# Layer 0's conditioning sums, all eight groups, split between TensorE's column quarters and VectorE

## Chip, cores and metric

The kernel runs on one NeuronCore of a Trainium2 chip. The metric is the device time of one execution in microseconds (us). Engines are named as in the profile: PE is TensorE's matmul, PEld its weight load, DVE is VectorE, ACT is ScalarE, POOL is GpSimd, SP is SyncE, which here only issues transfers.

## What is computed

A trunk of two layers over 256 tokens of width 2048. Each layer normalises its input twice, and each norm is scaled and shifted by vectors that come from a conditioning vector `c`:

```
cond = jax.nn.silu(c)
for l in range(DEPTH):
    mod = cond @ w_ada[l] + b_ada[l]
    shift1, scale1, gate1, shift2, scale2, gate2 = [m[:, None, :] for m in jnp.split(mod, 6, axis=-1)]
    h = rms_norm(x, norm1_w[l]) * (1.0 + scale1) + shift1
    mixed = mixer_groups(h, positions, w_in[l], ...)
    x = x + gate1 * (mixed @ w_out[l])
    h = rms_norm(x, norm2_w[l]) * (1.0 + scale2) + shift2
    gate_up = h @ w_ffn_in[l]
    ...
    x = x + gate2 * ((jax.nn.silu(g_ff) * u_ff) @ w_ffn_down[l])
return rms_norm(x, final_norm_w)
```

`cond @ w_ada[l]` is a vector of 2048 times a matrix of 2048 x 12288 in float32, 100 MB a layer. All sums are in float32.

## The kernel before

**The large products.** Every product with a large weight is made from two rounded parts of each operand, three matmuls in place of one. A piece of weights (256 rows, up to 512 columns) is loaded into `raw`, one of a ring of nine buffers, by SP; ACT rounds it to `whi` (L268), DVE takes the rest as `wlo` (L269), and PE runs it against `hTh` and `hTl`, the parts of the activations (L380, and L415 with the operands swapped). `fill` keeps LA = 3 pieces prepared ahead of PE; `hlp` has four buffers of each.

**The conditioning sums.** Before, they are no matmuls. For one group of a norm, `ada_pair` covers 512 of the 2048 columns, of the shift and of the scale together, so 1024 sums over 2048 rows. It takes 16 units, one for each 128 rows: unit `k` loads `raw` (128 x 2 x 512, 512 KB), and DVE adds `raw` times `cond[:, k]` to an accumulator `acc` (L443 for the first, L445 for the others). Then the 128 partitions must still be summed: `turn` transposes `acc` in eight blocks on PE (L472), `total_of` reduces on DVE (L478) and adds bias and norm weight (L479, L481). Four groups of a norm, two norms and two layers make 16 such groups. The gates (`ada_gate`, L441) go the same way and are not touched.

**The order.** All is written out in program order; an engine runs its own instructions in that order. Units wait in the queue `bg` and are popped between blocks (`pump`), at a rate set by when their group is due. The first norm of layer 0 has nothing to hide behind: its group 0 is run at once, all 16 units, with the start-up work between them (`setup`). Its groups 1 to 3 run beside the body of the group before: `first_groups` takes group g of the activations through eight column blocks of `w_in` (FIRST), and ahead of body g it calls `require`, which runs `at_once` of that group: the transposes, a `fill`, the reductions. Then `norm_steps` makes `hTh` and `hTl` on ACT (L606, L607) and DVE (L608), and the body starts with L415. The second norm's groups are deferred: their last steps are put between blocks some steps later (`later`).

**Start-up.** `c` is loaded as rows (`rowc`) and turned into columns by a transpose against the 128 x 128 identity `identt`; `silu` of it is `cond`. Transfers of SP and of ACT take semaphores from one ring of eight in turn, so a transfer waits until the one eight places before it in the ring has landed. Consts go through ACT's queue ahead of `cond`.

Of the kernel before, what the change touches and what calls it, by code (L numbers as in the profile page):

```python
# [19 lines left out]
P = 128  # L20
# [4 lines left out]
L = 2  # L25
# [9 lines left out]

LA = 3
NRAW = 9
NBIG = 24

CF = {}  # L40
_o = 0
# [39 lines left out]
def decoder(ctx: ExitStack, tc: tile.TileContext, x_d, c_d, pos_d, w_ada, b_ada, n1_d, w_in, w2_d, b2_d,  # L81
# [39 lines left out]
    nc.scalar.dma_start(identt, cf_d[:, CF["ident"][0]:CF["ident"][1]])  # L121
# [7 lines left out]
    load_rows(nc.scalar, lb_d, "lb")  # L129
    load_rows(nc.scalar, n1_d, "n1")  # L130
    brows = T2([P, P], n="brows")
    for l in range(L):
        for wh in range(2):
            o = 32 * (2 * l + wh)
            nc.scalar.dma_start(brows[o:o + 32],
                                b_ada[l, 6144 * wh:6144 * wh + 4096].rearrange("(r p) -> r p", p=P))
# [284 lines left out]

    def ada(l, c0, pair, finish, defer, dl):
        st = {}
        w = 512 if pair else 1024
        np_ = 1024 // w

        def unit(k):
            if k == 0:  # L430
                st["a"] = T4([P, np_, w], n="acc")
                if not pair:
                    G.memset(st["a"], 0.0)
                    nc.gpsimd.dma_start(st["a"][0:1, 0, :], b_ada[l:l + 1, c0:c0 + w])
            raw = rawp.tile([P, np_, w], F32, tag="raw", name=nm("raw"))
            rows_ = w_ada[l, k * P:(k + 1) * P, :]
# [5 lines left out]
            if pair and k == 0:  # L442
                V.tensor_scalar(out=st["a"], in0=raw, scalar1=cond[:, 0:1], scalar2=None, op0=ALU.mult)  # L443
            else:
                V.scalar_tensor_tensor(out=st["a"], in0=raw, scalar=cond[:, k:k + 1], in1=st["a"], op0=ALU.mult,  # L445
                                       op1=ALU.add)
            if k == KT - 1:
                if defer is None:
                    fill()
                    finish(st["a"])  # L450
                elif defer:
                    later.append([defer, None, lambda: finish(st["a"])])
                else:
                    finish(st["a"])

        for k in range(KT):
            bg.append((dl, lambda k=k: unit(k)))

    def ada_pair(l, which, g, dl, defer=6):
        base = 0 if which == 1 else 6144  # L460
# [13 lines left out]
        def total_of(j):  # L474
# [5 lines left out]
            if j:  # L480
                V.tensor_tensor(out=av[:, c], in0=s, in1=cols[:, r + 4 * g:r + 4 * g + 4], op=ALU.mult)  # L481
                done.add(key)

        def at_once(acc):
            turn(0, acc)
            turn(1, acc)
            fill(LA + 1 if g else LA)
            total_of(0)
            total_of(1)

        def fin(acc):
            def second():
                total_of(0)
                turn(1, acc)

            if defer:
# [8 lines left out]
        ada(l, base + 512 * g, True, fin, defer, dl)  # L505

    gates = {}

# [708 lines left out]
    def first_groups(act, nsteps, l, per_group):  # L1217
# [32 lines left out]
        for g in range(4):  # L1250
# [1 line left out]
            per_group(g)  # L1252
            next(nsteps)
            if g == 0:
                for _ in range(2):
# [39 lines left out]
    def at(W, r0, c0):  # L1295
        return where[W.offset, W.shape, r0, c0]

    for g in range(4):
        ada_pair(0, 1, g, at(w_in[0], g * 512, 4368), 0 if g else None)
    for l in range(L):  # L1300
        if l:
            for g in range(4):
# [5 lines left out]
        for h in range(2):  # L1308
            ada_gate(l, 2, h, at(w_fd[l], 0, 0) - 6)
    def setup():  # L1310
        yield from lower_bounds()
        yield
# [6 lines left out]
        yield  # L1319
        yield from trig()  # L1320

    his, los, xs = [], [], []
    prep = setup()
    for k in range(KT):
        bg.popleft()[1]()
        if k == 0:
            load_rows(nc.gpsimd, n2_d, "n2")
            load_rows(nc.gpsimd, b2_d, "b2")
# [4 lines left out]
        if k >= 2:  # L1333
            next(prep, None)
    nsteps = norm_steps(colv[0, "a1"], colv[0, "s1"], his, los, xs, False)

    def last_blocks(bs, adds, key, nsteps, xs):
# [207 lines left out]
```

## Time and profile before

| | |
|---|---|
| median of 3 runs | 2475.21 us (2473.01 to 2477.68) |
| profiled execution | 2479.04 us, its span 2477.2 us |
| busy over the span | PE 96%, DVE 72%, ACT 46%, POOL 4% |
| HBM read | 621.93 MB |
| instructions on PE (matmuls) | 11903 |

The profiled execution is 1.8 us longer than its span, and 3.8 us above the median of the runs. A busy PE in the profile is not PE at its peak, as the ends of pipelined matmuls are modelled; the pace of matmuls is read from the starts of following rows.

### The profile page before, as it was taken

The page shows a single profiled execution, that of the slowest core. Times are in us where ns is not written, and L with a number is a line of the kernel's source. Part 1 is how long each engine was busy: PE and PEld are TensorE (multiplying, and loading weights), DVE is VectorE, ACT ScalarE, POOL GpSimd, SP SyncE. Part 2 cuts the span into 40 slices and gives each one's busy share as a digit, 9 for nine tenths or more (in the row PEclk, how much of TensorE's full clock was granted, in tenths as well). Part 3 has the DMA queues.
Part 4 walks back from the last instruction along what each step waited for, and adds up shares of the span by engine and source line. Part 5 has one row for each costly group of instructions (what it writes and reads, how often), then busy time and mean ns, then how long its engine had stood idle before and what let it go on. Part 6 is the DMA issues. An engine that isn't in the chain of part 4 may idle for free.

```text
span 2477.2 us, 32091 instructions
## 1 busy us (share of the span) xinstructions
PE 2381.7 (96%) x11903; PEld 2007.2 (81%) x11903; DVE 1790.2 (72%) x2020; ACT 1129.3 (46%) x1560; POOL 99.1 (4%) x93
## 2 busy tenths in 40 slices
PE   2998989999999999999999999999999999999998
PEld 2887778878888888888879998888888888888886
DVE  6899899887777776777776787867876555455556
ACT  4434444455443344344455544554644344433444
POOL 0001220000000000000000111000000000000000
PEclk9999999999999999999999999999999999999999
DMA  8998689987888888888767776677787565555653
GB/s 310 362 340 295 184 262 311 313 290 281 299 280 295 285 273 277 281 274 298 270 224 246 245 227 213 226 233 260 257 277 268 203 194 182 186 196 193 194 199 108
DMA packets 314077, 626.16 MB, mean 253 GB/s; under 512 B 20276, under 2 KB 33568, under 8 KB 313664
## 3 DMA queue, kind: packets, MB, share of 16 engines
q1 hardware_dynamic: 312800, 622.68, 74.0%
q8 instruction: 93, 1.52, 0.3%
q10 hardware_dynamic: 720, 1.21, 0.1%
q14 instruction: 64, 0.52, 0.1%
q0 software_dynamic: 400, 0.22, 0.0%
HBM read 621.93 MB, written 2.10 MB: 252 GB/s over the span
## 4 chain that ended last, share of the span: by engine, by line
PE 74%; DVE 1%; ACT 1%; DMA 0%; issue 0%; ACTq 0%; DVEq 0%
PE d L380 66%; PE d L415 3%; PE d L398 1%; PE m L622 1%; PE m L380 1%; PE m L713 0%; PE m L719 0%; DVE wlo L269 0%; PE m L472 0%; ACT whi L268 0%; PE m L1003 0%; PE o L1045 0%; PE m L594 0%; PE m L885 0%; DMA raw<-in_w_in_dram 0%
## 5 line engine op out<-in xcount | busy, mean ns | idle before, releaser
L269 DVE TENSOR_TENSOR wlo<-raw,whi 128x1024 fp32r<-128x1024 f32 (+2 forms) x816 | 969.0, 1196 | 494.0 <-ACT whi L268 477.8
L268 ACT ACTIVATE whi<-raw 128x1024 fp32r<-128x1024 f32 (+2 forms) x816 | 833.9, 1036 | 779.1 <-PE d L380 646.1
L380 PE MATMUL d<-whi,hTh 128*128 128x512 f32 (+2 forms) x1880 | 503.3, 390 | 3.6 <-ACT whi L268 3.5
L380 PE MATMUL d<-whi,hTl 128*128 128x512 f32 (+2 forms) x1880 | 496.6, 384 | 0.0
L380 PE MATMUL d<-wlo,hTh 128*128 128x512 f32 (+2 forms) x1880 | 492.6, 384 | 0.0
L445 DVE SCALAR_TENSOR_TENSOR acc<-raw,cond,acc 128x1024 f32<-128x1024 f32 x368 | 478.7, 1301 | 7.1 <-DMA raw<-in_w_ada_dram 6.1
L380 PEld LDWEIGHTS d<-wlo,hTh 128*128 128x128 f32 x1880 | 348.8, 189 | 70.2
L380 PEld LDWEIGHTS d<-whi,hTl 128*128 128x128 f32 x1880 | 346.7, 189 | 68.8
L380 PEld LDWEIGHTS d<-whi,hTh 128*128 128x128 f32 x1880 | 341.0, 189 | 69.1 <-ACT whi L268 4.6
L380 PE MATMUL d<-whi,ah 128*128 128x512 f32 x672 | 180.9, 391 | 0.0
L380 PE MATMUL d<-whi,al 128*128 128x512 f32 x672 | 179.8, 389 | 0.0
L380 PE MATMUL d<-wlo,ah 128*128 128x512 f32 x672 | 179.7, 389 | 0.0
L380 PEld LDWEIGHTS d<-wlo,ah 128*128 128x128 f32 x672 | 126.2, 188 | 26.4
L380 PEld LDWEIGHTS d<-whi,al 128*128 128x128 f32 x672 | 126.1, 188 | 26.4
L380 PEld LDWEIGHTS d<-whi,ah 128*128 128x128 f32 x672 | 125.2, 188 | 25.3
L254 ACT ACTIVATE ah<-m 128x512 fp32r<-128x512 f32 x44 | 26.3, 598 | 102.7 <-PE m L622 102.7
L1442 ACT ACTIVATE sg<-d 128x512 f32<-128x512 f32 x44 | 23.9, 596 | 101.6 <-PE d L380 101.6
L1078 DVE TENSOR_TENSOR tmp<-d,gate 128x512 f32<-128x512 f32 x64 | 43.9, 686 | 31.8 <-PE d L380 20.5
L415 PE MATMUL d<-hTh,whi 128*128 128x256 f32 x320 | 50.3, 303 | 15.4 <-ACT hTh L606 15.3
L257 DVE TENSOR_TENSOR al<-m,ah 128x512 fp32r<-128x512 f32 x44 | 30.3, 689 | 46.1 <-ACT ah L254 46.1
L380 PE MATMUL d<-whi,mh 128*128 128x512 f32 x224 | 61.4, 395 | 1.7 <-DVE tmp L1078 1.7
L539 ACT ACTIVATE junk<-x 128x512 f32<-128x512 f32 x44 | 27.7, 630 | 75.1 <-DVE x L1079 75.1
(304 smaller groups left out, 2058.6 us busy)
## 6 DMA issues: line engine op xcount, KB each, us to landing
raw<-in_w_ada_dram SPq DMA_DIRECT2D x384, 512.0 KB, 5.4
raw<-in_w_ffn_in_dram SPq DMA_DIRECT2D x352, 512.0 KB, 4.8
raw<-in_w_in_dram SPq DMA_DIRECT2D x176, 512.0 KB, 5.4
raw<-in_w_ffn_down_dram SPq DMA_DIRECT2D x176, 512.0 KB, 4.9
raw<-in_w_out_dram SPq DMA_DIRECT2D x64, 512.0 KB, 5.5
raw<-in_w_in_dram SPq DMA_DIRECT2D x32, 256.0 KB, 3.6
raw<-in_w_in_dram SPq DMA_DIRECT2D x16, 272.0 KB, 4.1
x<-in_x_dram SPq DMA_DIRECT2D x2, 1024.0 KB, 7.3
```

The lines of the kernel that those rows point to most:

```text
L254: A.activation(hi, src, AF.Copy)
L257: V.tensor_tensor(out=lo, in0=src, in1=hi.bitcast(F32), op=ALU.subtract)
L268: A.activation(hi, raw, AF.Copy)
L269: lows.append(lambda: V.tensor_tensor(out=lo, in0=raw, in1=hi.bitcast(F32), op=ALU.subtract))
L380: TE.matmul(ps[t][:, :w], x4[:, k, t * P:(t + 1) * P], wp[:, kk], start=first and k + n == 0, stop=last and k == 3 and n == 2)
L398: TE.matmul(o, x4[:, k, t * P:(t + 1) * P], wp[:, kk], start=first and k + n == 0, stop=last and k == 3 and n == 2)
L415: TE.matmul(ps[f // 2][:, (f % 2) * S:(f % 2 + 1) * S], wp[:, kk, f * P:(f + 1) * P], x4[:, k], start=first and k + n == 0 and f % 2 == 0, ...
L445: V.scalar_tensor_tensor(out=st["a"], in0=raw, scalar=cond[:, k:k + 1], in1=st["a"], op0=ALU.mult, op1=ALU.add)
L539: A.activation(junk, xt[t][:, c * 512:(c + 1) * 512], AF.Square, accum_out=ssq[:, t, c:c + 1])
L622: TE.transpose(ps[:, h], y[:, h * P:(h + 1) * P], ident)
L1078: V.tensor_tensor(out=tmp, in0=ps, in1=gt, op=ALU.mult)
L1442: A.activation(s_, pg[t], AF.Silu)
```

## The change

For the eight groups of layer 0's two norms, part of the 16 units of a group goes to PE. `quarters` is a float32 matmul in four parts: the stationary operand is a column of `cond` widened to 32 columns by zeros (`wide[:, k]`), the moving operand a quarter of `raw` (256 of its 1024 columns), and the output of quarter j lies on PSUM partitions 32j to 32j + 31, so that it uses the array's columns 32j to 32j + 31. One call is one unit, called a set below. Its sum over the 128 rows is done by the matmul itself.

- Group 0 of the first norm (`first_group`): units 1, 3, 5, 7, 9 stay on DVE, the other eleven go to PE and accumulate in one PSUM bank; DVE's accumulator is added there by one more set against a column of ones.
- The other seven groups: units 1, 2, 6, 7, 11, 12 go to PE, in pairs. A pair is two sets that follow each other in a PSUM buffer of their own (a visit, below); DVE copies or adds its 128 x 256 result to `part` (L468, L470 of the changed kernel). Ten units stay on DVE. At the end one set against ones folds `acc` (`folded`), DVE adds `part` (`row_sums`), and `columns` turns the result with two transposes in place of eight and adds bias and weight with three short DVE operations.
- `cond` is made with a 16 x 16 identity loaded by itself, and the other consts are loaded behind it.
- The square sums of x come ahead of `lower_bounds` in `setup`; `setup` starts one unit later.
- Four units in place of two are popped at the start of body 0; one big buffer less (NBIG 23).

```
-NBIG = 24
+NBIG = 23
...
+    ident16 = con.tile([KT, KT], F32, name="ident16")
+    nc.scalar.dma_start(ident16, cf_d[0:KT, CF["ident"][0]:CF["ident"][0] + KT])
...
-    TE.transpose(cond_ps, rowc, ident[:KT, :KT])
+    TE.transpose(cond_ps, rowc, ident16)
     cond = con.tile([P, KT], F32, name="cond")
     A.activation(cond, cond_ps, AF.Silu)
+    wide = con.tile([P, KT + 1, 32], F32, name="wide")
+    parts2 = con.tile([P, 2, 256], F32, name="part")
+    V.memset(wide, 0.0)
+    V.tensor_copy(wide[:, 0:KT, 0], cond)
+    V.tensor_copy(wide[:, KT, 0:1], ones)
+    load_consts()
...
+    def quarters(ps, k, src, first, last):
+        for j in range(4):
+            TE.matmul(ps[32 * j:32 * j + 32, 0:256], wide[:, k], src[:, j // 2, (j % 2) * 256:(j % 2 + 1) * 256],
+                      start=first, stop=last)
...
+            if k in sum(own, ()):
+                part = parts2[:, g % 2]
+                at_pair = [p for p in own if k in p][0]
+                if k == at_pair[0]:
+                    st["raw"] = raw
+                else:
+                    ps = MB([P, 256])
+                    quarters(ps, at_pair[0], st.pop("raw"), True, False)
+                    quarters(ps, k, raw, False, True)
+                    if at_pair is own[0]:
+                        after_next.append(lambda: V.tensor_copy(part, ps))
+                    else:
+                        after_next.append(lambda: V.tensor_tensor(out=part, in0=part, in1=ps, op=ALU.add))
...
+        own = ((1, 2), (6, 7), (11, 12)) if (l, which) == (0, 1) or (l, which, g) in ((0, 2, 0), (0, 2, 1), (0, 2, 2), (0, 2, 3)) else ()
+
+        def folded(acc):
+            run_after()
+            st["ps"] = MB([P, 256])
+            quarters(st["ps"], KT, acc, True, True)
+
+        def row_sums():
+            st["rs"] = T2([P, 2, P], n="rs")
+            V.tensor_tensor(out=st["rs"].rearrange("p b n -> p (b n)"), in0=st["ps"], in1=parts2[:, g % 2], op=ALU.add)
...
         def at_once(acc):
+            if own:
+                folded(acc)
+                fill(LA + 1)
+                row_sums()
+                to_columns()
+                return
...
+    def first_group(prep):
+        ps = DB()
+        ops = ps[:, 0:256]
+        acc = [None]
+        own = (1, 3, 5, 7, 9)
...
+                if k == own[-1]:
+                    quarters(ps, KT, acc[0], False, False)
+            else:
+                quarters(ps, k, raw, k == 0, k == KT - 1)
```

What the order of instructions shows at three places. On SP, at the start of the program, before (`raw` are units of group 0, `x` the two halves of the input; DMAHW0 to 7 are the eight semaphores of the ring):

```order
L439 DMA raw_134<-in_w_ada_dram 128x2x512
L1332 DMA x_96<-in_x_dram 128x2048
L439 DMA raw_142<-in_w_ada_dram 128x2x512 [waits DMAHW2_49]
L1332 DMA x_97<-in_x_dram 128x2048 [waits DMAHW3_49]
L439 DMA raw_146<-in_w_ada_dram 128x2x512 [waits DMAHW4_49]
```

and of the change:

```order
L584 DMA raw_141<-in_w_ada_dram 128x2x512
L1434 DMA x_91<-in_x_dram 128x2048
L584 DMA raw_152<-in_w_ada_dram 128x2x512
L1434 DMA x_92<-in_x_dram 128x2048 [waits DMAHW2_49]
L584 DMA raw_157<-in_w_ada_dram 128x2x512 [waits DMAHW5_49]
```

The second unit's load waits for nothing now, and the second half of x waits for the small identity, which holds that semaphore.

On PE, from the end of start-up to the first matmul of body 0, before (the eight transposes of `acc`, then those of x; `d` is the body's PSUM):

```order
L472 MATMUL m_285<-identt,acc_133 128x128 x4
L472 MATMUL m_290<-identt,acc_133 128x128 x4
L594 MATMUL m_327<-identt,xs_202 128x128
L594 MATMUL m_327<-identt,xs_208 128x128
...
L415 MATMUL d_301<-hTh_325,whi_269 128x256 x2
```

and of the change, from the last sets of group 0 on:

```order
L437 MATMUL d_140<-raw_300,wide 32x256 x4
L437 MATMUL d_140<-raw_306,wide 32x256 x4
L696 MATMUL m_338<-identt,xs_195 128x128
L696 MATMUL m_338<-identt,xs_201 128x128
...
L488 MATMUL m_365<-identt,rs_363 128x128 x2
L437 MATMUL m_399<-raw_395,wide 32x256 x4
L437 MATMUL m_399<-raw_397,wide 32x256 x4
L426 MATMUL d_312<-hTh_336,whi_350 128x256 x2
```

The first pair of group 1 (`raw_395`, `raw_397`) now stands ahead of the body, so that PE can't start it before those two loads have landed.

On PE, in the output projection of layer 0, where the second norm's group 0 ends, before:

```order
L380 MATMUL d_3475<-wlo_3574,hTh_1278 128x512
L472 MATMUL m_3649<-identt,acc_2867 128x128 x4
L380 MATMUL d_3474<-whi_3605,hTh_1759 128x512
...
L380 MATMUL d_3475<-wlo_3606,hTh_1759 128x512
L472 MATMUL m_3680<-identt,acc_2867 128x128 x4
```

and of the change:

```order
L437 MATMUL m_3729<-raw_3697,wide 32x256 x4
L437 MATMUL m_3729<-raw_3727,wide 32x256 x4
L1140 MATMUL m_3739<-identt,sc_3560 128x128 x4
L1147 MATMUL o_3699<-sv_2950,pT_3707 128x64 x4
L391 MATMUL d_3610<-whi_3681,hTh_1376 128x512
...
L437 MATMUL m_3768<-acc_2913,wide 32x256 x4
```

PE's stream between the blocks holds a pair of sets and the fold, where it held two times four transposes.

## Rows read from the trace of the kernel before

**Rows 1.** By stretch: busy us of PE, PEld, DVE, ACT, POOL (instructions); clock, DMA share, GB/s.

```profile
50.00:100.00 50.00, 44.83 (x287) 41.23 (x287) 42.66 (x43) 27.95 (x46) 2.48 (x3) 0.97 0.92 319
600.00:650.00 50.00, 50.00 (x228) 41.34 (x227) 37.45 (x35) 22.55 (x27) 0.00 (x0) 1.00 0.89 316
```

**Rows 2.** Pace of body matmuls, timeline rows: start, us, instruction, count, wait.

```profile
64.17 1.07 PE L380 MATMUL m<-wlo,hTh 128*128 128x512 f32 x4
65.08 1.07 PE L380 MATMUL m<-whi,hTh 128*128 128x512 f32 x4
```

**Rows 3.** A piece of the chain that ended last: start, us, what, count.

```profile
738.11 81.65 PE d L380 x360
```

**Rows 4.** Timeline from start-up to the start of body 0.

```profile
35.87 1.06 ACT L268 ACTIVATE whi<-raw 128x1024 fp32r<-128x1024 f32 x1 [1.39 <-DMA raw<-in_w_in_dram]
36.42 6.56 DVE L445 SCALAR_TENSOR_TENSOR acc<-raw,cond,acc 128x1024 f32<-128x1024 f32 x5
...
48.89 2.13 PE L415 MATMUL d<-hTh,whi 128*128 128x256 f32 x8 [2.17 <-ACT hTh L606]
...
53.69 1.12 PE L415 MATMUL d<-hTh,whi 128*128 128x256 f32 x8
```

**Rows 5.** SP's waits, first 60 us, and transfer rates in 40 slices of 0 to 45 us.

```profile
SPq L439 <- DMA identt<-const_f_dram: 7.1, 1, 7.1
...
GB/s 0 42 171 426 372 412 256 27 31 275 401 386 370 393 406 401 388 388 388 386 384 393 386 382 386 393 382 386 390 390 382 350 259 302 328 271 351 333 257 364
```

**Rows 6.** Timeline at the boundary from body 0 to body 1.

```profile
91.19 1.04 PE L472 MATMUL m<-identt,acc 128*128 128x128 f32 x8
92.17 2.72 DVE L269 TENSOR_TENSOR wlo<-raw,whi 128x1024 fp32r<-128x1024 f32 x2 [0.63 <-ACT whi L268]
94.82 0.68 DVE L478 TENSOR_REDUCE sum<-m 128x4 f32<-128x512 f32 x1
...
96.52 0.16 DVE L481 TENSOR_TENSOR a<-sum,cols 128x4 f32<-128x4 f32 x1
...
97.40 2.13 PE L415 MATMUL d<-hTh,whi 128*128 128x256 f32 x8 [5.17 <-ACT hTh L606]
```

**Rows 7.** PE's waits at the next boundary, 130 to 160 us: in total, times, longest.

```profile
PE d L415 <- ACT hTh L606: 4.0, 1, 4.0
```

**Rows 8.** Timeline of float32 matmuls in layer 0's retention: four written, eight recorded.

```profile
448.96 1.89 PE L929 MATMUL m<-rqT,rkT 128*128 128x256 f32 x8
450.69 1.05 PE L933 MATMUL m<-rqT,rkT 128*128 128x128 f32 x8
```

**Rows 9.** Float32 matmuls on the whole array: the 16 and PE's next instruction.

```profile
236.20 1.95 PE L679 MATMUL m<-hq,hk 128*128 128x128 f32 x16
237.96 0.35 PE L380 MATMUL m<-whi,hTh 128*128 128x256 f32 x1
```

**Rows 10.** The same on halves of its rows, and the part within 306.60 to 306.72.

```profile
306.64 1.16 PE L679 MATMUL m<-gqk 64*128 64x128 f32 x16
307.74 0.74 PE L380 MATMUL d<-whi,hTh 128*128 128x256 f32 x4
...
306.64 0.38 PE L679 MATMUL m<-gqk 64*128 64x128 f32 x2
```

**Rows 11.** DVE by group: busy, mean ns of one, idle before.

```profile
L445 DVE SCALAR_TENSOR_TENSOR acc<-raw,cond,acc 128x1024 f32<-128x1024 f32 x368 | 478.7, 1301 | 7.1 <-DMA raw<-in_w_ada_dram 6.1
L1233 DVE TENSOR_TENSOR gg<-m,gg 128x256 f32<-128x256 f32 x12 | 4.9, 411 | 0.0
```

**Rows 12.** PE's waits, 200 to 350 us: first and last of six on DVE.

```profile
PE m L713 <- DVE kd L704: 3.9, 1, 3.9
...
PE m L380 <- DVE A L682: 0.2, 1, 0.2
```

**Rows 13.** PE's waits, 350 to 600 us: first and last of four on DVE.

```profile
PE d L380 <- DVE tmp L1078: 1.7, 1, 1.7
...
PE m L622 <- DVE y L635: 0.4, 1, 0.4
```

More of the change, by code (lines that the diff above doesn't have):

```diff
@@ L127, in load_rows, with load_consts @@
         q.dma_start(rows[ROWS[n]:ROWS[n] + r.shape[0]], r)
[L129 to L130 removed]
     brows = T2([P, P], n="brows")
[L132 to L136, printed above, removed]
+    def load_consts():
+        nc.scalar.dma_start(identt, cf_d[:, CF["ident"][0]:CF["ident"][1]])
+        load_rows(nc.scalar, lb_d, "lb")
+        load_rows(nc.scalar, n1_d, "n1")
+        for l in range(L):
+            for wh in range(2):
+                o = 32 * (2 * l + wh)
+                nc.scalar.dma_start(brows[o:o + 32],
+                                    b_ada[l, 6144 * wh:6144 * wh + 4096].rearrange("(r p) -> r p", p=P))
     bcols = con.tile([P, L * 2, 2, 16], F32, name="bcols")
@@ L457, in ada, with columns, pairs @@
             bg.append((dl, lambda k=k: unit(k)))
+    def columns(rs, l, which, g):
+        turned = MB([P, 2, P])
+        for b in range(2):
+            TE.transpose(turned[:, b], rs[:, b], ident)
+        got = turned.rearrange("p b (w j q) -> p w j b q", w=2, q=32)
+        sv, av, bias = colv[l, "s%d" % which], colv[l, "a%d" % which], bcols[:, 2 * l + which - 1]
+        c = slice(4 * g, 4 * g + 4)
+        def pairs(x):
+            return x.rearrange("p (j b) -> p j b", b=2)
+        t = SM([P, 10], n="sum")
+        V.tensor_tensor(out=pairs(t[:, 0:4]), in0=got[:, 1, :, :, 0], in1=pairs(bias[:, 1, c]), op=ALU.add)
+        V.tensor_tensor(out=pairs(sv[:, c]), in0=got[:, 0, :, :, 0], in1=pairs(bias[:, 0, c]), op=ALU.add)
+        r = ROWS["n1" if which == 1 else "n2"] + 16 * l + 4 * g
+        V.tensor_tensor(out=av[:, c], in0=t[:, 0:4], in1=cols[:, r:r + 4], op=ALU.mult)
     def ada_pair(l, which, g, dl, defer=6):
@@ L494, in second @@
                 turn(1, acc)
-            if defer:
+            if defer and own:
+                later.append([2, None, lambda: folded(acc)])
+                later.append([3, None, row_sums])
+                later.append([4, key, to_columns])
+            elif defer:
                 later.append([2, None, lambda: turn(0, acc)])
@@ L503, in fin, with finish @@
                 at_once(acc)
-        ada(l, base + 512 * g, True, fin, defer, dl)
+        ada(l, base + 512 * g, True, fin, defer, dl, own, g)
+    def first_group(prep):
[3 more added lines that the diff above has]
+        own = (1, 3, 5, 7, 9)
+        for k in range(KT):
+            raw = rawp.tile([P, 2, 512], F32, tag="raw", name=nm("raw"))
+            src = w_ada[0, k * P:(k + 1) * P, 0:2 * D].rearrange("p (j n) -> p j n", j=2)[:, :, 0:512]
+            nc.sync.dma_start(raw, src)
+            if k in own:
+                if acc[0] is None:
+                    acc[0] = T4([P, 2, 512], n="acc")
+                    V.tensor_scalar(out=acc[0], in0=raw, scalar1=cond[:, k:k + 1], scalar2=None, op0=ALU.mult)
+                else:
+                    V.scalar_tensor_tensor(out=acc[0], in0=raw, scalar=cond[:, k:k + 1], in1=acc[0], op0=ALU.mult,
+                                           op1=ALU.add)
+                if k == own[-1]:
+                    quarters(ps, KT, acc[0], False, False)
+            else:
+                quarters(ps, k, raw, k == 0, k == KT - 1)
+            prep(k)
+        def finish():
+            fill_high()
+            rs = T2([P, 2, P], n="rs")
+            V.tensor_copy(rs.rearrange("p b n -> p (b n)"), ops)
+            columns(rs, 0, 1, 0)
+            if lows:
+                lows.pop(0)()
+            done.add(("c", 0, 1, 0))
+        parked["c", 0, 1, 0] = finish
     gates = {}
@@ L1254, in first_groups @@
             if g == 0:
-                for _ in range(2):
+                for _ in range(4):
                     bg.popleft()[1]()
@@ L1296, in at @@
         return where[W.offset, W.shape, r0, c0]
-    for g in range(4):
-        ada_pair(0, 1, g, at(w_in[0], g * 512, 4368), 0 if g else None)
+    for g in range(1, 4):
+        ada_pair(0, 1, g, at(w_in[0], g * 512, 4368), 0)
     for l in range(L):
@@ L1319, in setup @@
         yield
+        yield from lower_bounds()
+        yield
         yield from trig()
@@ L1323, in decoder, with beside @@
     prep = setup()
-    for k in range(KT):
-        bg.popleft()[1]()
+    def beside(k):
         if k == 0:
```

20 lines of the change are left out of this document (9 added, 11 removed).

## The prediction, made before the changed kernel was run

> **What bounds the kernel now.** I read the busy time by stretch first. From 600 us on PE is busy all the time, 50.00 of 50 us, at a granted clock of 1.00, and DVE in 37.45; in 50 to 100 us PE has 44.83, DVE 42.66, and the transfers hold their engines for 0.92 of the time at 319 GB/s [rows 1]. So there are three stretches, and the question for each is which wait ends last.
>
> *From 350 us on* the chain that ended last is PE almost alone: 360 matmuls of 512 columns take 81.65 us, 0.2268 us each [rows 3]. PE's waits for DVE in 350 to 600 us are four, of together 3.4 us [rows 13]. Here whatever is added on PE is paid in full, and work taken off DVE can give back no more than those 3.4 us.
>
> *The bodies of layer 0's first norm* (49 to 200 us) look as if PE, DVE and the transfers were all at their limit. The pace tells them apart: four matmuls of 512 columns take 65.08 - 64.17 = 0.91 us, 0.2275 us each [rows 2], within half a percent of the pace at 738 us where nothing holds PE [rows 3]. So inside a body PE waits for nobody; DVE is full but hidden. PE stands still at the boundaries: 5.17 us ahead of body 1 [rows 6] and 4.0 ahead of each of bodies 2 and 3, of which one row stands here [rows 7].
>
> *Start-up* is the one place where the sums themselves are late. The first piece of `w_in`, loaded behind all 16 units, is on the chip by 35.87 us, when ACT takes it up as soon as it lands; DVE is still at its last five units, back to back, until 42.98; PE's transposes and the reductions can only follow, and body 0 starts at 48.89 [rows 4].
>
> **What it does to start-up.** Before, SP's third load waits 7.1 us, until the 64 KB identity has landed, and two slices of the rates, 2.25 us, hold almost nothing (27 and 31 GB/s) [rows 5]. Now that load waits for nothing, so I take 2.25 us off every landing behind it. I let the small consts, now issued behind `cond`, cost nothing: they share the eight semaphores with the units, and a unit that meets one still in flight issues late; what covers this is the backlog of loads already issued, which before kept the rate at 370 to 400 GB/s from the eleventh slice on. Without that cover the gap of 2.25 us comes back. The first piece of `w_in` then lands at 35.8 - 2.25, about 33.6. Eleven sets and a fold on PE replace eleven DVE operations of 1.30 us [rows 11]; the last six units are all PE's, each takes 0.43 us (below) or twice that at the lower clock, and loads come every 1.355 us (524288 bytes at some 387 GB/s [rows 5]), so PE keeps up and the sums end about 33. The tail (a copy of 128 x 256 at 0.41 us [rows 11], two transposes, three short operations) takes about 1.5 us, the third `w_in` piece lands at 33.6 + 2 x 1.355 = 36.3, and its rounding at 1.06 [rows 4] ends at 37.4. What is late next is a load: the first pair of group 1 stands ahead of the body on PE, and its second unit is the fifth load behind the first `w_in` piece: 33.6 + 5 x 1.355 = 40.4. With its set and the switch back, body 0 starts at about 41.1 in place of 48.89: **-7.8 us**. Queued behind that waiting set is the whole body.
>
> **What a set costs.** No matmul on column quarters stands in the trace. The nearest rows: a float32 matmul is recorded twice, and eight records of 256 columns take 450.69 - 448.96 = 1.73 us, 0.216 each [rows 8]. Four quarters are eight records: 1.73 us if they run one after the other, 0.43 if all four run side by side, 0.86 if two do. For row halves the trace has an answer. Sixteen records of 128 columns take 1.76 us on the whole array [rows 9] and 1.10 on halves, where two records start within the first 0.08 us [rows 10]: two truly run at once, 8 x 0.11 = 0.88 us, and 0.22 us is left over for going into the split array and back. I take the same for columns: **0.43 us a set and 0.22 us a visit**, so 1.08 for a pair and 0.65 for a fold. Both ends stay: 1.73 a set, and 0.43 with no switch.
>
> The Trainium skill ("TensorE: Matmul & The Clock Gate", Measured speedup vs the span model) gives 2.38 times for three column tiles of 32 at 512 columns, 0.79 of ideal; if four reach as much, a set is 1.73 / 3.17 = 0.55 us by that page, an estimate, and the sum rises by 0.12 for each of 40 sets, about 5 us. No run here shows columns yet. The page also says (The mechanism) that matmuls start and end strictly in program order, which speaks for the staircase of the first rival below; the two records of rows 10, which start together, don't bear it out.
>
> **What it does to the bodies.** Seven groups have three pairs; one pair has been counted in start-up. Eight visits in bodies 0 to 2, where PE waits for nobody: 8 x 1.08 = **+8.6 us**. The six DVE units taken away there (7.8 us a group) were hidden behind PE, and give nothing in the body. At a boundary, the stall is two `wlo` on DVE until 94.89 (they wait for ACT's rounding), then the reductions until 96.68 [rows 6], 1.8 us; in their place come one addition of 0.41, two transposes and three operations of 0.16, with two hops between engines, about 1.35: -0.45 each, **-1.4 us** for three. The fold takes the place of eight transposes ahead of those `wlo`, hidden by them. Body 1's stall is 1.2 us longer than the other two; I count no gain for it, and keep it as a bound.
>
> **What it does to the second norm.** Twelve visits between matmuls of layer 0's projections: 12 x 1.08 = +13.0. Four folds with two transposes each come for eight transposes of together 1.04 [rows 6]: 4 x (0.65 + 0.26 - 1.04) = -0.5. **+12.5 us**. DVE gets 6 x 1.30 + 2 x 0.68 - 4 x 0.41 = 7.5 us a group back, and may shorten the 3.4 us of waits; I take half, **-1.7**. A set also waits on PE for its own load, with all later blocks behind it. I cost this at nothing: DVE, which took these loads at the same place in the program, was kept waiting by them for 6.1 us in the whole run [rows 11]; without that slack each late load would add its delay. One of 24 large buffers less: nothing, bound unknown and small.
>
> **Sum**: -7.8 + 8.6 - 1.4 + 12.5 - 1.7 = +10.2 us on the profiled 2479.0. That execution is 3.8 us above the median of the runs, so I compare medians: 2475.2 + 10.2 = **2485**. About 0.2%, 5 us, is what the measurement can tell from no change.
>
> **Rivals.**
> - *Two quarters at a time.* If the two records of a quarter follow each other in order, the second must wait for the first on its columns, and only a staircase of two quarters overlaps. A set is 0.86, a pair 1.95, a fold 1.08: 8 x 1.95 + 12 x 1.95 + 4 x 0.30 = 40.2, start-up -7.4, boundaries and waits -3.1: +30, **2505**. For it too: four quarters read four different streams from the same partitions, which row halves don't. Against it: the two records that start together [rows 10].
> - *One after the other.* Pair 3.68, fold 1.95: 29.4 + 44.2 + 4.7 = 78.3, start-up about -6, the rest -3.1: +69, **2544**. The same doubt, further.
> - *Relief reaches the mixers.* In 200 to 350 us PE waits for DVE six times, 11.6 us in all [rows 12], and DVE carries units there. If DVE's 7.5 us a group empties that queue, these waits go, with all of the 3.4: 10.2 - 11.6 - 1.7 = -3.1, **2472**, and up to 8 us lower if PE, waiting less, also stays at the higher clock: the first eight L415 of body 0 take 2.13 us and later ones 1.12 [rows 4], which over two such rows at each of four starts is 8 us. It decides from about 10 us of relief on. Against it: only the second norm's first group can overlap that stretch; until then the gates' units, which are unchanged, run there.
> - *Start-up stays where it is*: the consts hold up the units' semaphores, or the last sets run late. +10.2 + 7.8 = +18.0, **2493**.
>
> **Chances.** Forecast 0.48, two at a time 0.18, one by one 0.07, relief 0.20, start-up 0.07. Within the forecast an error of some 6 us leaves 0.33 slower, 0.13 same, 0.02 faster; relief gives 0.14 faster, 0.06 same; the others are slower. Together: faster 0.16, same 0.19, slower 0.65. The range leaves out one by one, the worse part of two at a time, and the best of relief: 2466 to 2509. The forecast alone, with a switch of nothing to 0.3 us and a load that is late now and then, has 2480 to 2492.
>
> **What the next profile would show.** L437 with eight records in about 0.45 us, four starting together; a stretch of a pair from the last L391 to the next in about 1.1. Body 0's first L426 at 41 us, and in front of it the wait of L437 for a load. Boundaries of some 3.5 to 4.7 us. Bodies 1.08 us longer for each visit. From 350 to 600 us the waits about the same. I am wrong on the set if L437's records start one by one, on start-up if body 0 starts after 43 us, and on the hidden DVE if the waits in 200 to 350 us fall below 5 us.

## The result, and the profile after

The change makes the kernel slower: 2493.76 us median of 6 runs (2493.23 to 2494.28) against 2476.6 for the kernel before in the same session (2473.01 to 2478.47); the ratio is 1.0069, 95% interval 1.0059 to 1.0079. That is +17 us where +10.2 was forecast. The profiled execution took 2493.75 us, its span 2491.9.

By stretch, against [rows 1] (busy us of PE, PEld, DVE, ACT, POOL; clock, DMA share, GB/s), the changed kernel has:

```profile
50.00:100.00 50.00, 45.69 (x315) 39.20 (x314) 33.31 (x38) 25.76 (x41) 2.95 (x3) 0.94 1.01 360
600.00:650.00 50.00, 50.00 (x226) 41.39 (x225) 39.18 (x36) 22.10 (x25) 0.00 (x0) 1.00 0.94 340
```

DVE was given 9.4 of its 50 us back in the bodies, and PE has little of it: 28 matmul records more, and 4.3 us of idle time in place of 5.2.

**A set and a visit.** PE's timeline at the first pair inside a body. The first two rows are those of a window from 57.06 to 57.12 us, the others of 56 to 60:

```profile
56.88 0.28 PE L426 MATMUL d<-hTh,wlo 128*128 128x256 f32 x1
57.08 0.42 PE L437 MATMUL m<-raw,wide 128*32 128x256 f32 x4
...
57.08 1.07 PE L437 MATMUL m<-raw,wide 128*32 128x256 f32 x16
58.09 1.20 PE L391 MATMUL m<-whi,hTh 128*128 128x512 f32 x4
59.12 1.07 PE L391 MATMUL m<-whi,hTl 128*128 128x512 f32 x4
```

Four records start within 0.04 us: all four quarters run side by side. Two sets take 58.09 - 57.08 = 1.01 us, and the 0.20 from the start of the body's last matmul to theirs is 0.08 more than its own matmuls need (0.12 each in the changed kernel's records): 1.09, forecast 1.08. That isn't yet the whole visit. The four matmuls behind it take 59.12 - 58.09 = 1.03 us, where four take 0.91 [rows 2]: another 0.12, so that a pair costs **1.21** until the old pace is back, 0.35 of it for going in and out where the forecast had 0.22.

**Start-up.** SP's waits in the first 60 us (total, times, longest), the rates in 40 slices of 0 to 45 us, and the timeline to body 0, against [rows 4, 5]:

```profile
SPq L584 <- DMA raw<-in_w_ada_dram: 7.3, 5, 4.3
...
SPq L1434 <- DMA ident<-const_f_dram: 3.4, 1, 3.4
...
SPq L584 <- DMA rows<-in_hgrn_lb_dram: 2.9, 1, 2.9
```

```profile
GB/s 0 45 265 434 393 353 120 351 424 400 349 332 105 165 373 351 375 368 402 395 402 391 391 386 388 388 384 390 386 386 386 384 395 379 377 391 390 381 390 391
```

```profile
29.79 1.28 DVE L590 SCALAR_TENSOR_TENSOR acc<-raw,cond,acc 128x1024 f32<-128x1024 f32 x1
...
31.12 1.08 PE L437 MATMUL d<-acc,wide 128*32 128x256 f32 x8 [5.07 <-DVE acc L590]
...
31.98 4.88 PE L437 MATMUL d<-raw,wide 128*32 128x256 f32 x48
...
36.77 1.06 ACT L279 ACTIVATE whi<-raw 128x1024 fp32r<-128x1024 f32 x1 [3.41 <-DMA raw<-in_w_in_dram]
...
42.26 0.64 PE L437 MATMUL m<-raw,wide 128*32 128x256 f32 x8 [4.16 <-DMA raw<-in_w_ada_dram]
...
43.53 1.08 PE L437 MATMUL m<-raw,wide 128*32 128x256 f32 x8 [0.62 <-DMA raw<-in_w_ada_dram]
...
44.53 1.86 PE L426 MATMUL d<-hTh,whi 128*128 128x256 f32 x7
```

Body 0 starts at 44.53, 4.4 us earlier than before. The last thing ahead of it is the first pair of group 1, which waited 4.16 and 0.62 us for its two loads. The hole in the rates is not gone: it has become two (120, then 105 and 165), because SP now waits 3.4 us for the small identity, 2.9 for another const (`rows`) and up to 4.3 for an earlier unit.

**A boundary.** PE's timeline from body 1 to body 2 of the changed kernel, against [rows 6, 7]:

```profile
143.46 0.65 PE L696 MATMUL m<-identt,xs 128*128 128x128 f32 x4 [1.19 <-DVE gg L1335]
144.05 0.64 PE L437 MATMUL m<-acc,wide 128*32 128x256 f32 x8
146.89 0.69 PE L488 MATMUL m<-identt,rs 128*128 128x128 f32 x2 [2.20 <-DVE rs L536]
148.69 0.58 PE L426 MATMUL d<-hTh,whi 128*128 128x256 f32 x1 [1.11 <-ACT hTh L708]
```

The one wait of 4.0 us is now two of 2.2 and 1.1, and a wait for `gg` stands ahead of them.

**The second norm.** All of PE's waits for DVE from 350 to 600 us, against [rows 13]:

```profile
PE m L488 <- DVE rs L536: 0.9, 1, 0.9
PE d L409 <- DVE wlo L280: 0.8, 1, 0.8
PE m L673 <- DVE xs L657: 0.5, 1, 0.5
PE m L821 <- DVE part L470: 0.2, 1, 0.2
```

They are 2.4 us in place of 3.4. With the waits for ACT, which [rows 13] leave out, PE's waits in this stretch are 2.4 us in place of 5.4.

### The profile page after: what moved, and what is told of

Same layout as the page of the kernel before. It is cut to its first block, busy times and chain, and to the rows that moved or that the text cites. A ratio compares the mean times of both kernels' runs of the same rounds, so it can differ in the third digit from the quotient of the medians.

```text
span 2491.9 us, 32904 instructions
## 1 busy us (share of the span) xinstructions
PE 2413.0 (97%) x12343; PEld 2009.4 (81%) x12343; DVE 1728.9 (69%) x1983; ACT 1129.9 (45%) x1560; POOL 98.3 (4%) x93
## 3 DMA queue, kind: packets, MB, share of 16 engines
q10 hardware_dynamic: 752, 1.21, 0.1%
## 4 chain that ended last, share of the span: by engine, by line
PE 82%; DVE 2%; ACT 1%; DMA 0%; issue 0%; ACTq 0%; DVEq 0%
PE d L391 71%; PE d L426 3%; PE d L409 2%; PE m L724 1%; PE m L391 1%; DVE wlo L280 1%; PE m L815 0%; PE m L437 0%; PE o L1147 0%; PE m L1105 0%; ACT whi L279 0%; PE m L821 0%; PE m L515 0%; PE m L987 0%; DVE tmp L1180 0%
## 5 line engine op out<-in xcount | busy, mean ns | idle before, releaser
L474 DVE SCALAR_TENSOR_TENSOR acc<-raw,cond,acc 128x1024 f32<-128x1024 f32 x311 | 406.1, 1306 | 2.2 <-issue 1.5
L268 DVE TENSOR_TENSOR al<-m,ah 128x512 fp32r<-128x512 f32 x44 | 30.4, 690 | 45.8 <-ACT ah L265 45.8
L391 PE MATMUL d<-whi,ml 128*128 128x512 f32 x224 | 60.6, 391 | 0.0
```

The lines of the kernel that those rows point to most:

```text
L268: V.tensor_tensor(out=lo, in0=src, in1=hi.bitcast(F32), op=ALU.subtract)
L391: TE.matmul(ps[t][:, :w], x4[:, k, t * P:(t + 1) * P], wp[:, kk], start=first and k + n == 0, stop=last and k == 3 and n == 2)
```

## Experiments

The theory after this profile: each set and visit costs PE what was forecast and is paid in full; the start-up gain is cut by the pair in front of body 0 and by the loads. Rivals: the loss comes from the order of start-up and units; a visit's price is in something else than its sets; DVE or the loads are the real limit of the bodies. Medians of the kernel before in the later sessions are 2477.5 to 2478.1.

### 1 to 4: one half of the change at a time, and more sets

First group alone:

```
-        own = ((1, 2), (6, 7), (11, 12)) if (l, which) == (0, 1) or (l, which, g) in ((0, 2, 0), (0, 2, 1), (0, 2, 2), (0, 2, 3)) else ()
+        own = ()
```

> Only the first group of the first norm keeps TensorE's quarters; the other seven groups go back to VectorE's sums and the old transposes. Theory (each set on the quarters is paid in full by TensorE, and the start-up gains 4.4 us of the 7.8 forecast): body 0 starts at 43 to 45 us, and the time is about 2476.6 - 4.4 = 2472, 2470 to 2474. Rival (the loss comes from the new start-up order, the extra units popped ahead of body 0 or the missing big buffer, not from the visits): the time stays within 4 us of the change's 2493.8. Rival (start-up gain is given back at the first boundaries, where a group's sums were late before): 2475 to 2478.

First norm only (`... if (l, which) == (0, 1) else ()`):

> First norm (all four groups) on the quarters, second norm back on VectorE. Theory: the lag of the change against the kernel before went from -4.4 to about +6.2 us over bodies 0 to 2 and rose by 4.1 more between 200 and 350 us. If the rise between 200 and 350 us follows from work that the first norm pushed, 2476.6 + 10 = 2487; if it belongs to the second norm's units, 2483. Rival (visits cost nothing, VectorE's relief pays them): 2470 to 2474 as the first group alone.

First group and second norm (`... if (l, which) == (0, 2) else ()`):

> First group and the second norm's four groups on the quarters, groups 1 to 3 of the first norm back on VectorE. Theory: 2472 + 12 visits of 0.91 to 1.08 us + 4 folds = 2483 to 2486, and the sum of this run and the one with the first norm less the one with the first group alone gives the change's 2493.8 within 2 us. Rival (relief of VectorE between 350 and 600 us hides the second norm's visits): 2472 to 2475.

Two extra sets in each pair:

```
+                    quarters(ps, at_pair[0], st["raw"], True, True)
+                    quarters(ps, at_pair[0], st["raw"], True, True)
                     quarters(ps, at_pair[0], st.pop("raw"), True, False)
```

> As the change, but each of the 21 pair visits runs its first set of four quarters three times (the first two results are thrown away, the output is the same): 42 sets more. Theory (a set costs 0.43 us, all of it on the path): 2493.8 + 42 x 0.43 = 2511.9, 2509 to 2514. Rival (the four run two at a time: 0.86 us a set): 2530. Rival (a visit's price is the switch and the wait for its loads, the sets themselves lie in waits that are there anyway): under 2503.

| kernel | median us | ratio to before, interval |
|---|---|---|
| first group alone | 2479.91 | 1.0010 (1.0001 to 1.0019) |
| first norm | 2485.73 | 1.0044 (1.0030 to 1.0058) |
| first group and second norm | 2484.39 | 1.0031 (1.0019 to 1.0042) |
| change with 42 extra sets | 2510.23 | 1.0140 (1.0127 to 1.0154) |

The extra sets cost 2510.2 - 2493.8 = 16.4 us, 0.39 each, close to the 0.43 of the theory. In the trace of that kernel a visit of four sets takes 59.52 - 57.65 = 1.87 us, so that two sets more take 0.86:

```profile
57.65 1.93 PE L437 MATMUL m<-raw,wide 128*32 128x256 f32 x32
59.52 1.21 PE L391 MATMUL m<-whi,hTh 128*128 128x512 f32 x4
```

The second norm came out as expected. The first norm, at 2485.7, lies between its two expectations (2483 and 2487) and tells neither from the other. The first group alone was a miss: it should have gained 4 us and lost 2.4. Its first body starts 8.2 us earlier than before, and its second only 3.5 earlier (97.40 in [rows 6]). The two rows of its timeline:

```profile
40.69 0.74 PE L426 MATMUL d<-hTh,whi 128*128 128x256 f32 x4 [2.81 <-ACT hTh L708]
...
93.93 2.14 PE L426 MATMUL d<-hTh,whi 128*128 128x256 f32 x8 [6.17 <-ACT hTh L708]
```

The parts don't add up either: 2485.7 + 2484.4 - 2479.9 = 2490.2, not 2493.8, though runs of the first group alone spread from 2474 to 2484. This suggests that something all of these kernels share costs an amount that depends on the rest. They share the four units put ahead of body 0, the new order of start-up and one buffer less; experiments 5 and 9 change the first of these alone.

### 5 to 8: the units ahead, the visits, the loads and DVE

Two units ahead:

```
             if g == 0:
-                for _ in range(4):
+                for _ in range(2):
                     bg.popleft()[1]()
```

> As the change, but two units of group 1 instead of four are put ahead of body 0, so that no pair visit stands there. With the first group alone body 0 started at 40.7 us, with the change at 44.5. Theory (the 3.8 us between them are the pair ahead of body 0, which waited 4.2 and 0.6 us for its two loads): body 0 starts at 41 to 42 us. As the first group alone gave 4.7 of its 8.2 us back by body 1, the time follows only in part: 2491 to 2493. Rival (the pair is not what holds body 0; ScalarE's three roundings of w_in in front of hTh are): body 0 at 44 us and 2494.

It took 2489.48 us (ratio to before 1.0050, 1.0035 to 1.0065), 4.3 less than the change and more than expected. Body 0 starts where the pair no longer stands in the way:

```profile
41.42 2.13 PE L426 MATMUL d<-hTh,whi 128*128 128x256 f32 x8 [2.54 <-ACT hTh L708]
...
200.62 1.71 PE L426 MATMUL d<-hTh,whi 128*128 128x256 f32 x6 [1.11 <-ACT hTh L708]
```

Body 3, however, starts at 200.62 us with two units and at 200.52 with four. So in these traces the lead at the start was gone by then, and the 4.3 us come from the mixers and later. Two things eat it in body 0: the pair now stands inside it (1.21 us), and the granted clock was 0.53 in the first 6.6 us of the body (from 41.4 to 48), where the changed kernel had 0.76 (from 44.5 to 51).

Pairs split, so that the same 49 sets make 49 visits instead of 28:

```
-        own = ((1, 2), (6, 7), (11, 12)) if ...
+        own = ((1, 4), (6, 9), (11, 14)) if ...
...
                 if k == at_pair[0]:
-                    st["raw"] = raw
+                    st["ps2"] = MB([P, 256])
+                    quarters(st["ps2"], k, raw, True, False)
                 else:
-                    ps = MB([P, 256])
-                    quarters(ps, at_pair[0], st.pop("raw"), True, False)
+                    ps = st.pop("ps2")
                     quarters(ps, k, raw, False, True)
```

> As the change, but the two sets of each pair are issued in two units three apart, into one PSUM tile: the same 49 sets in 49 visits instead of 28. Theory (a visit costs a switch of 0.22 us besides its sets): 2493.8 + 21 x 0.22 = 2498.4, 2496 to 2500. Rival (the switch costs nothing, sets alone count): 2493 to 2495. Rival (the switch is dear, 0.5 us or more): over 2504.

It took 2506.06 us (1.0115, 1.0100 to 1.0131): 12.3 us for 21 visits, 0.58 each, as the rival with a dear switch had it. The timeline gives part of that: a visit of one set takes 64.36 - 63.79 = 0.57 us, and it starts 1.00 us after the first of four matmuls that need 4 x 0.2275 = 0.91 [rows 2], so 0.09 more: 0.66, forecast 0.65. The four matmuls behind it, however, take 65.79 - 64.36 = 1.43 us in place of 0.91. Behind a pair inside the bodies that row was 0.12 too long; here it is 0.4 longer still, for a reason that no run shows.

```profile
62.79 1.07 PE L391 MATMUL m<-wlo,hTh 128*128 128x512 f32 x4
63.79 0.64 PE L437 MATMUL m<-raw,wide 128*32 128x256 f32 x8
64.36 1.59 PE L391 MATMUL m<-whi,hTh 128*128 128x512 f32 x4
65.79 0.40 PE L391 MATMUL m<-whi,hTl 128*128 128x512 f32 x1
```

At 0.35 for each of 21 switches 7.4 of the 12.3 us are accounted for. PE also has a wait of 4.3 us for `hg` from 45 to 200 us that the changed kernel has not, but others are shorter: all its waits there are 12.3 us against 12.7. From 200 to 600 us they are 23.1 against 19.2, which covers 3.9 of the other 4.9. A split pair holds one of the small PSUM buffers over three units; whether that causes waits was not tried by itself.

Two kernels ask what limits the bodies of the first group alone. One leaves out every second load of groups 1 to 3 (DVE reads the tile before a second time):

```
+            skip = pair and l == 0 and c0 < 2048 and k % 2
+            raw = st["raw0"] if skip else rawp.tile([P, np_, w], F32, tag="raw", name=nm("raw"))
```

> The first group alone on the quarters, and for groups 1 to 3 of the first norm every second load of 512 KB is left out (VectorE reads the tile before again: as many sums, wrong ones). With the first group alone body 0 started 8.2 us early and body 1 only 3.5 us early. Theory (in bodies 0 to 2 the loads are the limit: their share was 1.03 to 1.07 from 50 to 80 us): the lead is kept, body 1 starts at 89 to 91 us instead of 93.9, and the time falls by 3 to 6 us to 2474 to 2477. Rival (VectorE, busy 9.9 of 10 us from 50 to 70 us, is the limit): body 1 at 93 to 94 us and about 2479.9.

The other leaves out every second of DVE's sums there:

```
+            elif pair and l == 0 and c0 < 2048 and k % 2:
+                V.tensor_copy(junk1, raw[:, 0, 0:1])
```

> The first group alone on the quarters, and for groups 1 to 3 of the first norm every second of VectorE's sums (1.3 us) is replaced by a copy of one column; all loads stay. Theory (the loads are the limit of bodies 0 to 2): body 1 at 93 to 94 us and about 2479.9. Rival (VectorE is the limit there): body 1 at 89 to 91 us and 2474 to 2477. If both this and the halved loads help by half, each holds the other up.

Busy time from 50 to 90 us of the first group alone, then with half the loads, then with half the sums:

```profile
50.00:90.00 40.00, 35.68 (x227) 31.82 (x225) 36.89 (x34) 20.32 (x30) 0.49 (x1) 1.00 1.01 359
```

```profile
50.00:90.00 40.00, 34.94 (x226) 31.64 (x224) 39.65 (x40) 18.24 (x29) 2.09 (x3) 1.00 0.85 267
```

```profile
50.00:90.00 40.00, 36.01 (x220) 32.41 (x219) 25.74 (x32) 20.09 (x30) 0.04 (x1) 0.96 1.01 362
```

Body 1 with half the loads, then with half the sums:

```profile
90.58 2.14 PE L426 MATMUL d<-hTh,whi 128*128 128x256 f32 x8 [5.43 <-ACT hTh L712]
```

```profile
94.41 0.80 PE L426 MATMUL d<-hTh,whi 128*128 128x256 f32 x2 [6.05 <-ACT hTh L710]
```

What ACT waits for from 41 to 88 us, in the first group alone and with half the loads:

```profile
ACT whi L279 <- DMA raw<-in_w_in_dram: 21.3, 14, 2.7
```

```profile
ACT whi L279 <- DMA raw<-in_w_in_dram: 2.9, 3, 1.6
```

Body 0 of the first group alone is limited by the loads: with the load share down to 0.85 it keeps 6.8 of its 8.0 us, though DVE works 39.65 of the 40 us, and ACT hardly waits for `w_in` any more. With DVE down to 25.74 of 40 it keeps 3.0, and ACT still waits 16.0 us for `w_in`; some 1.6 us of the loss there can be the granted clock, 0.96 over these 40 us. The total did not follow: 2477.78 us (0.9999, 0.9990 to 1.0008) and 2477.62 (1.0004, 0.9994 to 1.0013). Both are 2 us below the first group alone, which its own spread of 10 us does not tell from nothing. The lead that the half loads kept through body 0 is lost later, so the loads are not all of it.

### 9 to 12: the order of units, the identity, the fold

First group alone with two units ahead (both edits above):

> The first group alone on the quarters, and two units ahead of body 0 as in the kernel before (the first group alone had four). Theory (the four units shift every later unit of VectorE by two places, and in the mixers the shifted order loses 3 to 4 us: all runs with four lost that between 205 and 345 us, the one with two lost nothing): the lead at body 3 of 2.6 to 3.5 us is kept through the mixers, and the time is 2477.5 - 3 = 2474, 2471 to 2476; it beats both kernels. Rival (the mixers are tied to something that does not move with the start, so any lead is lost there): 2477 to 2481.

It took **2471.67 us** (2468.8 to 2473.4), ratio 0.9979, 0.9969 to 0.9988: faster than both kernels, as expected. All loads and all sums are there, and the lead holds: from its timeline, body 0 at 40.14, body 1 at 91.09 and body 3 at 187.57 us, where the first group with four units had 40.69, 93.93 and 192.86.

```profile
40.14 0.74 PE L426 MATMUL d<-hTh,whi 128*128 128x256 f32 x4 [1.54 <-ACT hTh L708]
...
91.09 2.14 PE L426 MATMUL d<-hTh,whi 128*128 128x256 f32 x8 [6.10 <-ACT hTh L708]
...
187.57 2.13 PE L426 MATMUL d<-hTh,whi 128*128 128x256 f32 x8 [3.98 <-ACT hTh L708]
```

The same number alone, in the kernel before:

```
-                for _ in range(2):
+                for _ in range(4):
```

> The kernel before with one number changed: four units ahead of body 0 instead of two, all sums on VectorE, the start-up as it was. Theory (the shifted order of units): it is slower by 3 to 4 us from the mixers, plus what the two more units cost ahead of body 0 (2 x 1.3 us of VectorE at most): 2480 to 2484, and PE's waits for kd and gg between 215 and 350 us are those of the runs with four. Rival (the order is indifferent): 2477.5, 2476 to 2479.

2481.87 us (1.0021, 1.0012 to 1.0030), +4.1: the size expected, not the place. Body 1 starts at 98.86, 1.5 late, and body 3 at 197.69, some 2.3 later than before; the mixers took the rest, not all of it. Rows of its timeline:

```profile
98.86 1.49 PE L415 MATMUL d<-hTh,whi 128*128 128x256 f32 x5 [6.22 <-ACT hTh L606]
...
197.69 1.71 PE L415 MATMUL d<-hTh,whi 128*128 128x256 f32 x6 [3.98 <-ACT hTh L606]
```

The kernel before with the small identity and the new order of the consts alone:

```
+    ident16 = con.tile([KT, KT], F32, name="ident16")
...
-    TE.transpose(cond_ps, rowc, ident[:KT, :KT])
+    TE.transpose(cond_ps, rowc, ident16)
...
+    load_consts()
```

> The kernel before with the small identity and the new order of the constant loads alone; all of the first group's sums on VectorE and eight transposes as before. Theory: cond comes 3.1 us earlier, so VectorE's sums and body 0 start about 3 us earlier (45.5 to 46.5 us instead of 48.9), and about half of it is kept by body 1: 2475 to 2477. Rival (the quarters are not needed for the start-up: the loads of w_in set it): body 0 at 41 to 42 us, as with the first group's quarters. Rival (VectorE's work for the constants, now behind the squares of x, falls behind the sums): body 0 at 49 us or later, 2477 to 2480.

2478.12 us (1.0002, 0.9993 to 1.0011), no change. DVE's 16 sums still end at 42 us and body 0 starts at 47.92, 1.0 earlier; neither the 3 us of the theory nor the 41 of the rival. So the small identity and the new order do little alone, and it is the quarters in the first group that move the start.

```profile
42.06 1.97 PE L478 MATMUL m<-identt,acc 128*128 128x128 f32 x8 [26.58 <-DVE acc L451]
...
47.92 2.14 PE L421 MATMUL d<-hTh,whi 128*128 128x256 f32 x8 [2.18 <-ACT hTh L612]
```

Experiment 9 with the fold at the boundaries and no visits:

```
-            V.tensor_tensor(out=st["rs"].rearrange("p b n -> p (b n)"), in0=st["ps"], in1=parts2[:, g % 2], op=ALU.add)
+            V.tensor_copy(st["rs"].rearrange("p b n -> p (b n)"), st["ps"])
...
         def at_once(acc):
-            if own:
+            if (l, which) == (0, 1):
```

> As the first group alone with two units ahead (2471.7), and for groups 1 to 3 of the first norm all 16 sums stay on VectorE, so there are no visits, but at the boundary the finished sum is folded by one set of quarters, copied, and turned by two transposes, in place of eight transposes and two reductions. Theory (the boundary term of the forecast, -0.45 us each, can be had without the visits): 2471.7 - 1.4 = 2470.3, and the stretch from the last transposes of the normed x to the next body's first product is 0.3 to 0.9 us shorter at each of the three boundaries. Rival (the fold's wait for VectorE's copy takes it back: the change waited 2.2 to 3.1 us for its row sums): 2471.5 to 2474.

2472.19 us (0.9982, 0.9973 to 0.9991), not to be told from experiment 9. Boundaries are 0.2, 0.6 and 0.6 us shorter from the last transposes of x to the next body, together the 1.4 us that the forecast gave them, but the time doesn't show it; the second one goes from 133.57 to 139.11 there, and here:

```profile
134.42 0.66 PE L696 MATMUL m<-identt,xs 128*128 128x128 f32 x4 [0.56 <-DVE gg L1335]
...
139.40 0.96 PE L426 MATMUL d<-hTh,whi 128*128 128x256 f32 x3 [1.11 <-ACT hTh L708]
```

## Why the prediction was right in sign and short in size

Experiments 9 and 5 divide the loss. The median goes from 2477.8 (before) to 2471.7 (first group on the quarters, two units ahead), to 2489.5 (all groups, two units ahead), to 2493.8 (four units ahead): **-6.1, +17.8, +4.3**, together +16.0 (+17.2 against the runs of the first session). The forecast had -7.8 for the first group, +18.0 for the other seven, and nothing for the units ahead. The shares depend on the order in which the parts are added: with the four units put in before the seven groups they are -6.1, +8.2 and +13.9.

**A set at 0.43: right; a visit at 0.22: too little.** The extra sets measured 0.39 to 0.43 each, and both rivals with slower sets are out: that records start in order does not keep four from running side by side. Up to the next matmul a pair measured 1.09 and a visit of one set 0.66, as forecast. The forecast left out that the matmuls behind a visit need 0.12 us to get back to their pace, so a pair is 1.21 and the switch 0.35. Against the 1.73 us of eight records that follow each other [rows 8], four quarters side by side run 4.0 times as fast; with its switch a pair runs 3.46 / 1.21 = 2.9 times as fast. The Trainium skill ("TensorE: Matmul & The Clock Gate", Measured speedup vs the span model) gives 2.38 for three column tiles, from which the prediction estimated 0.55 a set; here the measurement decides, and it is 0.43.

**Start-up, -7.8: measured -4.4.** The step that failed is "I take 2.25 us off every landing behind it. I let the small consts [...] cost nothing". The consts do hold SP back, as the text had named it: the holes of the rates are still there, and the first piece of `w_in` is taken up at 36.77, forecast 33.6 and 0.9 later than before. The step behind it held to a tenth: the pair's second load is the fifth behind that piece, and 36.77 + 5 x 1.355 = 43.5, where L437 started at 43.53. The set there took 1.00 us to the body's first matmul, at a granted clock of 0.50, where the forecast allowed 0.65. Two more steps were off and cost nothing: the sums ended at 36.8, not 33, because the fold waited 5.07 us for unit 9 on DVE, which stood behind `setup`'s work, and the six sets behind it took 0.80 us each. What stands behind them was not ready before 41.4: that is where body 0 starts when no pair stands ahead of it (experiment 5), and there it waits for ACT.

**Bodies, +8.6 - 1.4: measured +9.5.** From the start of body 0 to that of body 3 the changed kernel takes 200.52 - 44.53 = 156.0 us, the kernel before 195.43 - 48.89 = 146.5. Body 3 in the kernel before, then in the changed kernel:

```profile
195.43 2.13 PE L415 MATMUL d<-hTh,whi 128*128 128x256 f32 x8 [3.97 <-ACT hTh L606]
```

```profile
200.52 1.71 PE L426 MATMUL d<-hTh,whi 128*128 128x256 f32 x6 [1.11 <-ACT hTh L708]
```

Eight visits at 1.21 are 9.7 us. The boundaries themselves, from the last transposes of x on, are shorter by 0.9, 0.3 and 0.6 us, together 1.8, as forecast. What was missed is the wait for `gg` in front of those transposes, 3.0 us in two in the changed kernel, 0.8 in the kernel before: it gave the gain back. It belongs to the four units ahead, as the rows below show.

**Second norm, +12.5 - 1.7: less.** It costs 4.5 us beside the first group alone (2484.4 - 2479.9) and 8.1 beside the whole first norm (2493.8 - 2485.7). Both terms were too small, and the errors cancel. Twelve pairs at 1.21 are 14.5 us. From the first norm alone to the whole change PE's waits from 45 to 2400 us fall by 6.9 us (45.8 to 38.9 in the traces), where the forecast took 1.7 for DVE's relief: 7.6, near the 8.1. Beside the first group alone they fall by only 3.9, which leaves 10.6 where 4.5 was measured. There the runs also differ in granted clock (median 0.989, and 0.9915 with the second norm); what that is worth no run shows.

**The missing term.** The four units ahead of body 0 stand in the diff and had no price in the sum apart from the pair's wait. They cost 4.3 us in the changed kernel (2493.8 - 2489.5), 4.1 in the kernel before and 8.2 with the first group alone (2479.9 - 2471.7). The other seven groups cost +17.8, near the 19.1 that the forecast's terms give once the ninth pair too is counted in the bodies, but that is luck in part: 21 pairs at 1.21 are 25.4 us, and PE's waits from 45 to 2400 us are 8.6 us shorter in experiment 5 than in experiment 9 (36.0 and 44.6), where the forecast took 3.1 for all reliefs. So, by the first order above, this term and 1.7 us of the start-up are why +10.2 became +16 to +17.

**Which part of that is shown.** That the number of units ahead is the cause is shown three times, by changing nothing else. All four runs of the change with two units lie below all six with four, if only just (2493.1 and 2493.2). Through what it acts is shown in part. PE's waits for `gg` from 45 to 200 us, with two units and then with four, of the kernel before, of the first group alone and of the change:

```profile
PE m L594 <- DVE gg L1233: 0.8, 2, 0.5
```

```profile
PE m L594 <- DVE gg L1233: 2.8, 2, 1.5
```

```profile
PE m L696 <- DVE gg L1335: 0.8, 2, 0.6
```

```profile
PE m L696 <- DVE gg L1335: 2.8, 2, 1.5
```

```profile
PE m L696 <- DVE gg L1335: 0.5, 1, 0.5
```

```profile
PE m L696 <- DVE gg L1335: 3.0, 2, 1.8
```

Each time four units add 2.0 to 2.5 us of it. All of PE's waits from 45 to 350 us grow by 3.9 (31.2 to 35.1), 6.2 (30.2 to 36.4) and 4.6 us (24.9 to 29.5), beside 4.1, 8.2 and 4.3 in the medians. From 200 to 350 us alone its waits for DVE are 13.4 us in the changed kernel, 12.2 with two units, and 11.6 in the kernel before [rows 12]. These are single profiles, and the one of the first group alone lies 3.0 us above its median, the one of experiment 9 2.9 below, so the medians carry the sizes and the traces only the place. Which unit of DVE delays which of `gg`, `kd` and `hg` was not tried. In body 0 of the first group alone the loads are a limit with two units too: ACT waits 21.0 us for `w_in` there, 21.3 with four. That body is 2.3 us longer with four, and 1.7 of that can be the granted clock, 0.79 against 1.00 from 40 to 48 us. *Relief reaches the mixers* did not happen; its test, waits below 5 us, failed clearly at 13.4.

**Start-up as a source of gain: right.** *Start-up stays where it is* gave the nearest number, 2493, for a reason that holds in part: the start moved by half, and the rest was lost to the units. With two units and the first group alone the time falls by 6.1 us for a body that starts 8.8 us earlier.

## What to carry to other kernels

Work that is hidden behind the bound engine costs little where it is; moved onto that engine, it costs its price there, and here shorter waits gave back only a third of it (8.6 of 25.4 us). Move only the part whose end something waits for: here the first of eight groups, which gained 6 us, while the other seven lost 14 to 18. Price a switch until the old pace is back, not until the next instruction starts. And price the one-number edits: how many units of a background queue are run ahead shifts each load and each operation behind them, and here that was worth 4 to 8 us, as much as the start-up was meant to gain.

## What the hardware showed that was not expected

- Four float32 matmuls on 32 columns each, with four different moving operands of 256 columns, ran with no loss: 8 records in 0.43 us, where eight on the whole array take 1.73.
- Coming back from the quarters costs something too: the four matmuls of 512 columns behind a pair took 1.03 us, where four take 0.91 [rows 2].
- The six sets behind the fold in start-up took 4.81 / 6 = 0.80 us each, and those in the bodies 0.43. PE had stood still for 5.07 us before the fold. The view gives a granted clock of 1.00 for 32 to 36.5 us, but this trace's record of the clock begins only at 36.25, so whether these sets ran at the lower of the two levels no row shows. The set ahead of body 0, at a recorded 0.50, took 1.00 us to the next matmul, where one takes 0.57 inside a body.
- The transfers' share was 0.94 to 1.01 from 50 to 90 us with all loads, at 331 to 362 GB/s: a stretch can have PE, DVE and the loads all near their limit, and only taking half of one away told which holds the others.
